# The r gate product token-major by one level of Strassen's algorithm, ahead of the branch gates

## The chip, the cores and the metric

The kernel runs on one core of one Trainium2 chip. The metric is the time of one execution on the device in microseconds (us), the median of several runs; smaller is better. The core has five engines with a queue each: PE (TensorE, matrix products and transposes; PEld is its loading of the stationary operand), DVE (VectorE), ACT (ScalarE), POOL (GpSimd) and SP (SyncE). Each engine works its instructions off in order. Matrix products read from SBUF and write to PSUM, in banks of 128 x 512 floats; DVE and ACT read PSUM. Loads from DRAM are issued here by SP, and by POOL and ACT in places.

## The reference, cut to what matters

One layer of a token mixer and a channel mixer over 512 tokens of width 1024, in fp32. `h` is the input x, normalised by its RMS and modulated by a vector computed from c (`w_ada`). One wide product `z = h @ w_in` is split into u, vs, q, r, ga, gb, k, v, lr. Then:

```python
a = _spatial_gating(gelu(u), gelu(vs), ...)          # u * (vs, normalised, mixed over tokens by sgu_w)
o, s_f, s_b = _gla_bidir(qh, k, v, lr, ...)           # gated linear attention, 4 heads of 256 values
o = o * lax.rsqrt(jnp.mean(o * o, axis=-1, keepdims=True) + EPS)
o = o.reshape(...) * gla_norm_g
ob = o * jax.nn.silu(r)
merged = jax.nn.sigmoid(ga) * (a @ w_br_a) + jax.nn.sigmoid(gb) * (ob @ w_br_b)
return merged @ w_o
```

The channel mixer follows: norm and modulation, `w_up` (44 blocks of 128 columns), a depthwise convolution over the token grid, gelu gate, `w_down`. The change concerns r, a 512 x 1024 by 1024 x 1024 product, and what is made of it, `ob`.

## The kernel before, in words

*Products.* An fp32 operand is split into a rounded part `h` and a rest `l`, both of type fp32r, and a product is three: high by high, high by low, low by high. `prod_cm` makes one block of 128 output columns for all 512 tokens, channel-major (channels on the partitions, tokens along the row): 8 slices of the inner dimension by 3 = 24 matmuls of 128x512 into one bank (L366). `wide_tm` makes blocks token-major, 128 tokens by 512 channels (L384). Activations in channel-major form (`hx` for the modulated x, 8 pairs; `a_act`; `ob`; `mg`) are the inputs of both.

*Weights.* All weights pass through one stream, in the order of the list `specs`: SP loads a raw block of 512 KB (`stream_load`, L220, 4 buffers), ACT casts it to `wh` (L232) and DVE subtracts to get `wl` (L233; 5 buffers of each). `weights()` hands out the next block and issues the splits and loads of those after it. A block is a 128-column strip with all 1024 rows, or, for the token-major products, 256 rows by 512 columns.

*Opening.* SP loads x, then, in turn, the first half of `w_ada` in groups (L282) and the first weights. For each group PE multiplies by the columns of c and c_ctx (L569), a small product sorts the result (L578), DVE makes scale and shift of it, and ACT and DVE modulate the transposed x with them (L599, L600) and split it into `hx`. Meanwhile PE already runs the first products with the parts of `hx` that are there (L660). POOL loads small rows and the decay weights (`rest_load`, L309 to L313). All of this is kept in written order.

*Stages around the change*, by the start of their products: VS (vs, token-major, `wide_tm`), U (246 us), GA/BRA (302 us: ga block, then the product of `a` with `w_br_a`, eight times), R (394 us), GB/BRB (439 us), `w_o` (524 us), the up product and convolution of the FFN (583 us) and its down product (812 us). The last is already done by Strassen's algorithm: seven products of quarters (L1554) whose weight sums POOL builds in DRAM by DMAs, plain and accumulating (`sums_build`, L201 and L203), one step with each call of `weights()` from weight 60 (`SUMS0`) on.

*U.* For each j: the product, gelu on ACT (L1226), and one step later `sgu_part`: four matmuls of 128x128 (two passes each, L1213) of the normalised vs (`vsn`, made by 32 operations on DVE, L1143) with the mixing weights, then two DVE operations (L1215, L1217) and the split of `a` (L358, L359). Between them stand, for each head, `o_scale` (the RMS factor on o, L1152) and `o_turn`: 8 transposes of 128x128 of o (L1158) and, on ACT, the factor `gng` (L1161) into a channel-major tile `ot`.

*R.* For each j a product of `prod_cm`, sigmoid on ACT (L1262), two multiplications on DVE (L1263 by `ot`, L1264 by r itself), and the split into `ob` (L358, L359).

*ada2* computes the second half of the modulation vector on DVE: 64 times a loaded tile of `w_ada` (256 KB, on SP, L1181) times a column of c, added up (L1182). It is cut into 88 steps; `tick(n)` does n of them. It starts in U; each product of U, GA/BRA, R and GB/BRB does `tick(2)`.

*Pools.* `heap` has 44 tiles of 2 KB per partition, `late` 27; PSUM has 4 banks `mm` and 4 banks `gl`. A tile that is asked for waits until the one that had its place is no longer read. The framework's scheduler sets the order of each engine's queue from the program, with some stretches kept in written order.

Of the kernel before, what the change touches and what calls it, by code (L numbers as in the profile page):

```python
# [20 lines left out]
KT = 8  # L21
# [13 lines left out]
SUMS0 = 60  # L35
# [3 lines left out]
def backbone_kernel(  # L39
# [98 lines left out]
    def w_cols(w, c0, n=P, k0=0, kn=KT):  # L138
        specs.append((w[k0 * P:(k0 + kn) * P, c0:c0 + n].rearrange("(k p) c -> p k c", p=P), kn, n))
# [24 lines left out]
    for f in range(FT):  # L164
        w_cols(ffn_w_up[0], f * P)
        w_cols(ffn_w_up[0], FF + f * P)
    quarter = lambda b, row, col: ffn_w_down[0][(4 * b + 2 * row) * P:(4 * b + 2 * row + 2) * P,
                                                 col * 512:(col + 1) * 512]
    sums = [[dp.tile([2 * P, 576], F32, name=nm("sum"))[:, :512] for _ in range(4)]
            for _ in range(BLOCKS)]  # L170

    def w_block(ap):
        specs.append((ap.rearrange("(k p) c -> p k c", p=P), 2, 512))

# [17 lines left out]
    def sums_build():  # L192
        for step in (((0, (0, 1)), (1, (1, 1)), (2, (1, 0)), (3, (0, 1))), ((0, (0, 0)), (3, (1, 1))),
                     ((1, 0),), ((2, 1),)):
            for b in range(BLOCKS):
# [14 lines left out]
    building = sums_build()  # L210
# [39 lines left out]
    def weights():  # L250
        i = pos[2]
        pos[2] += 1
        if i >= SUMS0:
            next(building, None)
        stream_split(i + 2)
        stream_load(i + 1 + AHEAD)
        return splits.pop(i)
# [519 lines left out]
    in_order(STRICT, T.engine, A.engine, V.engine)  # L777
    lsb = [heap([P, S], F32R, s="lsb") for _ in range(2)]
# [333 lines left out]
    vsn = [heap([P, 4, P], s="vsn") for _ in range(8)]  # L1112
# [28 lines left out]
    for g in range(8):  # L1141
        for t in range(4):
            V.tensor_scalar(vsn[g][:, t, :], vraw[g // 4][t][:, (g % 4) * P:(g % 4 + 1) * P], mv[:, t, 0:1],  # L1143
                            vrs[:, t:t + 1], op0=ALU.subtract, op1=ALU.mult)


    o_t = []

    def o_scale(h):
        for t in range(4):  # L1150
            ov = o_tok[h][t // 2][:, t % 2, :]
            V.tensor_scalar(ov, ov, ors[:, h, t:t + 1], None, op0=ALU.mult)  # L1152

    def o_turn(h):
        for hv in range(2):
            ps = gl()
            for t in range(4):
                T.transpose(ps[:, t * P:(t + 1) * P], o_tok[h][t // 2][:, t % 2, hv * P:(hv + 1) * P], ident)  # L1158
            t_ = late([P, S], s="ot")
            j = 2 * h + hv  # L1160
            A.mul(t_, ps, gng[:, j:j + 1])  # L1161
            o_t.append(t_)
# [42 lines left out]
    bg.append(ada2())  # L1205


    a_act = []

    def sgu_part(j, ug):  # L1210
        ps = gl()
        for t in range(4):
            T.matmul(ps[:, t * P:(t + 1) * P], vsn[j][:, t, :], swT[j // 4][:, j % 4, :], start=True, stop=True)  # L1213
# [4 lines left out]
        a_act.append(split_act(ug, s="a"))  # L1218

    prev = None  # L1220
    for j in range(KT):
        w = weights()
# [10 lines left out]
        if j < NH:  # L1233
            o_scale(j)
        if 0 < j <= NH:
            o_turn(j - 1)
        tick(2)
# [3 lines left out]
    t1, ob = [], []  # L1241
    for j in range(KT):
# [5 lines left out]
        tick(2)  # L1248
# [5 lines left out]
        tick(2)  # L1254


    for j in range(KT):
        w = weights()
        ps = mm()
        prod_cm(ps, w, hx)  # L1260
        sr = heap([P, S], s="sr")
        A.activation(sr, ps, AF.Sigmoid)  # L1262
        V.tensor_tensor(sr, o_t[j], sr, op=ALU.mult)  # L1263
        V.tensor_tensor(sr, ps, sr, op=ALU.mult)  # L1264
        ob.append(split_act(sr, s="ob"))
        tick(2)
# [3 lines left out]
    for j in range(KT):  # L1270
# [5 lines left out]
        tick(2)  # L1276
# [5 lines left out]
        mg.append(split_act(sgb_, s="mg", lo_pool=late))  # L1282
        tick(2)
# [386 lines left out]
```

## Time and profile before

| | before |
|---|---|
| median of 3 runs | 925.48 us (925.4 to 925.8) |
| profiled execution: span | 925.1 us |
| profiled execution: its own time | 928.11 us |
| granted TensorE clock | 0.998 |
| PE / DVE / ACT / POOL busy | 910.6 / 683.8 / 403.6 / 42.5 us |
| moved by DMA | 140.76 MB, 152 GB/s in the mean |

The profile is one execution, recorded by the hardware. Its times start with the first instruction; its own time is the whole execution's and includes what lies before and after the span. A row of a group reads: line, engine, operation, what it writes <- what it reads, shape, count | busy us in all, mean ns of one | idle time of the engine before them, and what ended most of it. A row of waits reads: who waits <- for whom: us in all, times, longest. A row of the chain reads: start, length, engine and line, count. A row of windows reads: stretch, its length, busy time of PE, PEld, DVE, ACT and POOL (count), granted clock, busy share of the DMA engines, GB/s. A row of one line or tile reads: line, engine, operation, count: shortest/median/longest ns, first and last start in us, shape. Matmuls are pipelined: a duration of theirs overlaps the next one's.

### The profile page before, as it was taken

The numbers are of one execution on the slowest core, as the hardware profiler recorded it, in microseconds if no ns is written. First come the engines' busy times: TensorE is split into PE (matmuls) and PEld (weight loads), VectorE is DVE, ScalarE is ACT, GpSimd is POOL, SyncE is SP. The second block draws the span as 40 slices with busy tenths as digits, with TensorE's granted clock in tenths as the row PEclk, the third lists the DMA queues.
The fourth block names the chain that finished last, engine by engine and source line by source line (L and its number), as shares of the span: only waits on it lengthen the run. The fifth ranks groups of instructions, "written<-read, shape, count | busy, mean of one in ns | idle before, by whom it ended". The sixth has DMA issues, their size and how long they took to land.

```text
span 925.1 us, 12162 instructions
## 1 busy us (share of the span) xinstructions
PE 910.6 (98%) x4540; PEld 760.5 (82%) x4540; DVE 683.8 (74%) x1187; ACT 403.6 (44%) x673; POOL 42.5 (5%) x74
## 2 busy tenths in 40 slices
PE   7999999999999999999999999999999999999996
PEld 5778888888888888888888889888888888888885
DVE  5578687779799653498575446898787778998966
ACT  5357465556542332222233236633333334467633
POOL 1200000000000000000000110011111000000000
PEclk9999999999999999999999999999999999999999
DMA  8940400511417653484444681688989632356552
GB/s 266 353 149 28 134 24 1 176 52 47 125 59 232 195 186 92 126 286 120 149 162 157 205 301 48 196 219 173 215 177 204 141 109 92 103 173 202 160 159 91
DMA packets 158615, 140.76 MB, mean 152 GB/s; under 512 B 6825, under 2 KB 122869, under 8 KB 158557
## 3 DMA queue, kind: packets, MB, share of 16 engines
q1 hardware_dynamic: 149197, 117.72, 41.1%
q0 software_dynamic: 8672, 21.19, 10.3%
q10 hardware_dynamic: 688, 1.09, 0.3%
q8 instruction: 35, 0.57, 0.2%
q14 instruction: 23, 0.19, 0.1%
HBM read 137.88 MB, written 23.07 MB: 174 GB/s over the span
## 4 chain that ended last, share of the span: by engine, by line
PE 97%; DMA 1%; ACT 0%; SPq 0%; DVE 0%; issue 0%; ACTq 0%
PE mm L366 56%; PE mm L384 12%; PE gl L1554 9%; PE gl L890 3%; PE mm L660 2%; PE mm L1554 1%; PE gl L660 1%; PE mm L997 1%; PE mm L1047 1%; PE gl L384 1%; PE gl L569 1%; PE gl L925 1%; PE gl L1213 1%; DMA wa<-in_w_ada_dram 1%; PE gl L366 1%; PE mm L377 1%
## 5 line engine op out<-in xcount | busy, mean ns | idle before, releaser
L232 ACT CAST wh<-raw 128x1024 fp32r<-128x1024 f32 x154 | 161.8, 1054 | 319.9 <-PE mm L366 204.7
L233 DVE TENSOR_TENSOR wl<-raw,wh 128x1024 fp32r<-128x1024 f32 x154 | 187.1, 1221 | 92.0 <-ACT wh L232 91.3
L366 PE MATMUL mm<-h2l,wh 128*128 128x512 f32 (+1 forms) x344 | 133.0, 387 | 0.0
L366 PE MATMUL mm<-h2h,wh 128*128 128x512 f32 (+1 forms) x344 | 133.0, 387 | 0.0
L366 PE MATMUL mm<-h2h,wl 128*128 128x512 f32 (+1 forms) x344 | 133.0, 387 | 0.0
L1401 DVE SCALAR_TENSOR_TENSOR cacc<-ca,ccol,cacc 128x441 f32<-128x441 f32 (+2 forms) x176 | 121.8, 694 | 4.1
L366 PE MATMUL mm<-hxh,wh 128*128 128x512 f32 x296 | 116.1, 392 | 0.0
L366 PE MATMUL mm<-hxl,wh 128*128 128x512 f32 x296 | 115.4, 390 | 0.0
L366 PE MATMUL mm<-hxh,wl 128*128 128x512 f32 x296 | 115.4, 390 | 0.0
L366 PEld LDWEIGHTS mm<-h2l,wh 128*128 128x128 f32 x344 | 64.6, 188 | 13.2
L366 PEld LDWEIGHTS mm<-h2h,wh 128*128 128x128 f32 x344 | 64.6, 188 | 13.2
L366 PEld LDWEIGHTS mm<-h2h,wl 128*128 128x128 f32 x344 | 64.6, 188 | 13.0
L366 PEld LDWEIGHTS mm<-hxh,wl 128*128 128x128 f32 x296 | 55.6, 188 | 11.6
L366 PEld LDWEIGHTS mm<-hxh,wh 128*128 128x128 f32 x296 | 55.6, 188 | 11.2
L366 PEld LDWEIGHTS mm<-hxl,wh 128*128 128x128 f32 x296 | 55.6, 188 | 11.2
L1182 DVE SCALAR_TENSOR_TENSOR acc<-wa,cs,acc 128x512 f32<-128x512 f32 x64 | 46.0, 744 | 3.2 <-DMA wa<-in_w_ada_dram 3.2
L1554 PE MATMUL gl<-wh,dah 128*128 128x512 f32 x120 | 46.7, 389 | 0.0
L1554 PE MATMUL gl<-wl,dah 128*128 128x512 f32 x120 | 46.7, 389 | 0.0
L1554 PE MATMUL gl<-wh,dal 128*128 128x512 f32 x120 | 46.7, 389 | 0.0
L1402 ACT ACTIVATE cacc<-cacc 128x512 f32<-128x512 f32 x22 | 13.9, 632 | 50.1 <-DVE cacc L1401 50.1
L384 PE MATMUL mm<-wh,hxh 128*128 128x512 f32 x88 | 34.7, 394 | 0.0
L384 PE MATMUL mm<-wl,hxh 128*128 128x512 f32 x88 | 34.4, 391 | 0.0
(425 smaller groups left out, 1678.8 us busy)
## 6 DMA issues: line engine op xcount, KB each, us to landing
raw<-in_w_in_dram SPq DMA_DIRECT2D x52, 512.0 KB, 3.8
wa<-in_w_ada_dram SPq DMA_DIRECT2D x96, 256.0 KB, 4.9
raw<-in_ffn_w_up_dram SPq DMA_DIRECT2D x44, 512.0 KB, 4.3
sum<-in_ffn_w_down_dram POOLq DMA_DIRECT2D x30, 512.0 KB, 6.0
raw<-sum SPq DMA_DIRECT2D x20, 512.0 KB, 3.8
raw<-in_ffn_w_down_dram SPq DMA_DIRECT2D x17, 512.0 KB, 3.5
sum<-sum POOLq DMA_DIRECT2D x10, 512.0 KB, 7.3
raw<-in_w_br_a_dram SPq DMA_DIRECT2D x8, 512.0 KB, 5.3
```

The lines of the kernel that those rows point to most:

```text
L232: A.copy(wh, raw)
L233: V.tensor_tensor(wl, raw, wh.bitcast(F32), op=ALU.subtract)
L366: T.matmul(ps, a[:, k, :], b[:, c0:c0 + n], start=(k == 0 and i == 0), stop=(k == KT - 1 and i == 2))
L377: T.matmul(ps, a[:, k, :], b[:, c0:c0 + n], start=(k == 0 and i == 0), stop=(k == KT - 1 and i == 2))
L384: T.matmul(ps, a[:, t * P:(t + 1) * P], b[:, k % 2, :], start=(k == 0 and i == 0), stop=(k == KT - 1 and i == 2))
L569: T.matmul(aps[32 * j:32 * j + 32, :cg], cs[:, k, :], wa[2 * (k // nk) + kind][:, k % nk, :], start=(k < 2), stop=(k >= KT - 2), tile_posi ...
L660: T.matmul(fps[i], a, b, start=(k == 0 and z == 0), stop=(k == KT - 1 and z == 2))
L890: T.matmul(ps, p_, q_, start=(start and z == 0), stop=(stop and z == 2))
L1182: V.scalar_tensor_tensor(acc[j], w_, cs[:, k, 0:1], acc[j], op0=ALU.mult, op1=ALU.add)
L1401: V.scalar_tensor_tensor(o, a_[:, r0 + dy:r1 + dy, c0 + dx:c1 + dx], wcol(tap), o, op0=ALU.mult, op1=ALU.add)
L1402: A.activation(acc, acc, AF.Gelu)
L1554: T.matmul(ps, a, w[:, kk, c0:c0 + n_], start=(first and kk == 0 and i == 0), stop=(last and kk == 1 and i == 2), skip_group_check=True)
```

## The change

- r is computed token-major by one level of Strassen's algorithm: the 512 x 1024 by 1024 x 1024 product is cut into two blocks of the inner dimension, each block's operands into quarters; seven products (`r_product`), each over both blocks, in place of eight. One product is 2 banks (token tiles of 128) x 2 blocks x 2 slices x 3 matmuls of 128x512 = 24. Results go to `rX` (2 banks of `mm`), `rZ` (2 of `gl`), `rY` (2 of `mm`); `taken` copies a result out on ACT, `combine` adds two on DVE.
- Its weights are 14 blocks of 256 x 512; half of them are sums of quarters that POOL builds in DRAM (a second list of 16 DMA steps of the same `sums_build`, from weight 2 on, i.e. during the attention heads and VS). For r they stand between those of U and GA.
- The sums of the other operand: each modulated tile of x (`fx`) is stored to DRAM by POOL in the opening stage; in U `hx_sum` loads quarters of it on SP (16 loads of 128 KB), adds or subtracts them on DVE and splits them.
- The RMS factor, the gate and o are combined token-major: `r_gate` does a sigmoid on ACT, two DVE operations of 128x256 (o times its factor times the sigmoid) and one of 128x512 (times r). `ob_turn` transposes the result (16 transposes for each half of the channels), multiplies by `gng` on ACT and takes the rest on DVE: that gives `ob`. `o_scale` and `o_turn` go.
- `vsn` becomes 8 operations of 128x512 in place. The high halves of `a` and `mg` are cast on ACT instead of DVE.
- R moves ahead of GA/BRA. `ada2` starts after it, with `tick(3)` in GA/BRA and GB/BRB alone. `SUMS0` is 66, since six weight blocks more stand ahead of it; the place in the program is the same.

PE at the end of r: before, r's first product follows the last of BRA's (`mm_4003`), 24 matmuls to a bank:

```order
L366 MATMUL mm_4003<-ah_3382,wh_3946 128x512
L366 MATMUL mm_4003<-al_3383,wh_3946 128x512
L366 MATMUL mm_4003<-ah_3382,wl_3947 128x512
L366 MATMUL mm_4003<-ah_3400,wh_3946 128x512
L366 MATMUL mm_4003<-al_3401,wh_3946 128x512
L366 MATMUL mm_4003<-ah_3400,wl_3947 128x512
L366 MATMUL mm_4041<-hxh_430,wh_3997 128x512
L366 MATMUL mm_4041<-hxl_431,wh_3997 128x512
L366 MATMUL mm_4041<-hxh_430,wl_3998 128x512
L366 MATMUL mm_4041<-hxh_485,wh_3997 128x512
L366 MATMUL mm_4041<-hxl_486,wh_3997 128x512
L366 MATMUL mm_4041<-hxh_485,wl_3998 128x512
```

Now GA's first product follows r, and with it stand transposes of the gated tiles (`obt`) into `gl` banks, of which the third set waits for the bank of the first:

```order
L379 MATMUL mm_3708<-hxl_546,wh_3622 128x512
L379 MATMUL mm_3708<-hxh_545,wl_3623 128x512
L379 MATMUL mm_3708<-hxh_605,wh_3622 128x512
L1289 MATMUL gl_3670<-ident,obt_3468 128x128
L1289 MATMUL gl_3670<-ident,obt_3475 128x128
L1289 MATMUL gl_3670<-ident,obt_3606 128x128
L1289 MATMUL gl_3670<-ident,obt_3611 128x128
L379 MATMUL mm_3708<-hxl_606,wh_3622 128x512
L1289 MATMUL gl_3679<-ident,obt_3468 128x128
L1289 MATMUL gl_3679<-ident,obt_3475 128x128
L1289 MATMUL gl_3679<-ident,obt_3606 128x128
L1289 MATMUL gl_3679<-ident,obt_3611 128x128
```

The transposes of o, which stood between U's products, now lie here and after BRA's first product; r is over before GA begins.

DVE in r: before, the gate's operations and splits alternate with `ada2`'s (`acc`):

```order
L1182 SCALAR_TENSOR_TENSOR acc_3982<-wa_868_4077,cs,acc_3982 128x512
L233 TENSOR_TENSOR wl_4216<-raw_4129,wh_4215 128x1024
L1263 TENSOR_TENSOR sr_4066<-ot_3021,sr_4066 128x512
L1182 SCALAR_TENSOR_TENSOR acc_3985<-wa_876_4119,cs,acc_3985 128x512
L1264 TENSOR_TENSOR sr_4066<-mm_4041,sr_4066 128x512
L1182 SCALAR_TENSOR_TENSOR acc_3988<-wa_877_4122,cs,acc_3988 128x512
L358 CAST obh_4070<-sr_4066 128x512
L1182 SCALAR_TENSOR_TENSOR acc_3979<-wa_885_4164,cs,acc_3979 128x512
L359 TENSOR_TENSOR obl_4071<-sr_4066,obh_4070 128x512
L1182 SCALAR_TENSOR_TENSOR acc_3982<-wa_886_4167,cs,acc_3982 128x512
L1263 TENSOR_TENSOR sr_4111<-ot_3028,sr_4111 128x512
```

Now, at the end of r, the last gates (`obt`), the splits of GA's and BRA's weights (`wl`), the rests of `ob_turn` and the last two combinations stand in this order:

```order
L245 TENSOR_TENSOR wl_3703<-raw_3620,wh_3702 128x1024
L1281 TENSOR_TENSOR obt_3611<-mm_3345,obt_3611 128x512
L245 TENSOR_TENSOR wl_3757<-raw_3626,wh_3756 128x1024
L245 TENSOR_TENSOR wl_3834<-raw_3706,wh_3833 128x1024
L245 TENSOR_TENSOR wl_3876<-raw_3760,wh_3875 128x1024
L1292 SCALAR_TENSOR_TENSOR obl_3658<-gl_3652,vec_b,obh_3657 128x512
L1292 SCALAR_TENSOR_TENSOR obl_3667<-gl_3661,vec_b,obh_3666 128x512
L1292 SCALAR_TENSOR_TENSOR obl_3676<-gl_3670,vec_b,obh_3675 128x512
L1292 SCALAR_TENSOR_TENSOR obl_3685<-gl_3679,vec_b,obh_3684 128x512
L1302 TENSOR_TENSOR dc_3688<-gl_3346,dt_3516 128x512
L1302 TENSOR_TENSOR dc_3695<-gl_3347,dt_3518 128x512
L1279 SCALAR_TENSOR_TENSOR obt_3690<-o_2133,var,obt_3690 128x256
```

`ada2` is gone from this stretch, and two weight splits that take the buffers of r's last product stand ahead of the first `obl`.

SP in U: before, the weights of the coming products and `ada2`'s loads:

```order
L220 DMA raw_3109<-in_w_in_dram 128x8x128
L220 DMA raw_3178<-in_w_in_dram 128x8x128
L220 DMA raw_3243<-in_w_in_dram 128x8x128
L1175 DMA acc_2935<-in_b_ada_dram 1x512
L1175 DMA acc_2938<-in_b_ada_dram 1x512
L1175 DMA acc_2941<-in_b_ada_dram 1x512
L1175 DMA acc_2944<-in_b_ada_dram 1x512
L1181 DMA wa_647_2947<-in_w_ada_dram 128x512
```

Now U's and r's weights with the first quarters of `fx` between them:

```order
L1223 DMA fq_2895<-fx_974 128x256
L1223 DMA fq_2895<-fx_976 128x256
L232 DMA raw_3141<-in_w_in_dram 128x8x128
L232 DMA raw_3191<-in_w_in_dram 128x2x512
L232 DMA raw_3241<-in_w_in_dram 128x2x512
L232 DMA raw_3291<-sum_135 128x2x512
L232 DMA raw_3354<-sum_139 128x2x512
L232 DMA raw_3360<-in_w_in_dram 128x2x512
L1223 DMA fq_3120<-fx_978 128x256
```

The loads of `ada2` have left this stretch, and the quarters' loads stand ahead of U's last weight.

The diff, cut to its core:

```diff
+    R_AT = len(specs)
...
-    for j in range(KT):
-        w_cols(wi, O_R + j * P)
...
+    quarter, sums = quarters(ffn_w_down[0], 0), sum_tiles(BLOCKS)
+    r_quarter, r_sums = quarters(wi, O_R), sum_tiles(2)
+    down_specs, specs = specs, []
+    for f in (lambda b: r_quarter(b, 0, 0), lambda b: r_sums[b][0], lambda b: r_quarter(b, 1, 0),
+              lambda b: r_sums[b][1], lambda b: r_sums[b][3], lambda b: r_sums[b][2],
+              lambda b: r_quarter(b, 1, 1)):
+        for b in range(2):
+            w_block(f(b))
+    down_specs[R_AT:R_AT] = specs
+    specs = down_specs
...
-    building = sums_build()
+    building = {SUMS0: sums_build(quarter, sums), 2: sums_build(r_quarter, r_sums)}
...
+    fx_kept = []
+    for k in range(KT):
+        d = dp.tile([P, S], F32, name=nm("fx"))
+        G.dma_start(d, fx[k])
+        fx_kept.append(d)
...
-    for g in range(8):
+    for hf in range(2):
         for t in range(4):
-            V.tensor_scalar(vsn[g][:, t, :], vraw[g // 4][t][:, (g % 4) * P:(g % 4 + 1) * P], mv[:, t, 0:1],
-                            vrs[:, t:t + 1], op0=ALU.subtract, op1=ALU.mult)
+            z = vraw[hf][t]
+            V.tensor_scalar(z, z, mv[:, t, 0:1], vrs[:, t:t + 1], op0=ALU.subtract, op1=ALU.mult)
...
+    def hx_sum(b):
+        def quad(i, hf):
+            t_ = heap([P, 2, 256], s="fq")
+            for kk in range(2):
+                dma(t_[:, kk], fx_kept[4 * b + 2 * i + kk][:, hf * 256:(hf + 1) * 256])
+            return t_
+
+        def kept(name, t_, p, q, op):
+            V.tensor_tensor(t_, p, q, op=op)
+            pair = [pool([P, 2, 256], F32R, s="xs") for pool in (heap, late)]
+            A.copy(pair[0], t_)
+            V.tensor_tensor(pair[1], t_, pair[0].bitcast(F32), op=ALU.subtract)
+            hx_sums[name, b] = pair
...
+    def r_gate(hf, t, src):
+        z = late([P, 512], s="obt")
+        A.activation(z, src, AF.Sigmoid)
+        for hh in range(2):
+            h = 2 * hf + hh
+            zh = z[:, hh * 256:(hh + 1) * 256]
+            V.scalar_tensor_tensor(zh, o_tok[h][t // 2][:, t % 2, :], ors[:, h, t:t + 1], zh,
+                                   op0=ALU.mult, op1=ALU.mult)
+        V.tensor_tensor(z, src, z, op=ALU.mult)
+        ob_t[hf, t] = z
+
+    def ob_turn(hf):
+        for jj in range(4):
+            j = 4 * hf + jj
+            ps = gl()
+            for t in range(4):
+                T.transpose(ps[:, t * P:(t + 1) * P], ob_t[hf, t][:, jj * P:(jj + 1) * P], ident)
+            hi, lo = heap([P, S], F32R, s="obh"), late([P, S], F32R, s="obl")
+            A.mul(hi, ps, gng[:, j:j + 1])
+            V.scalar_tensor_tensor(lo, ps, gng[:, j:j + 1], hi.bitcast(F32), op0=ALU.mult, op1=ALU.subtract)
+            ob[j] = (hi, lo)
...
+    def r_product(banks, ops, first=False):
+        zs = [(weights(), a) for a in ops]
+        for t in range(2):
+            for b, ((wh, wl), (hi, lo)) in enumerate(zs):
+                for kk in range(2):
+                    for i, (a, w) in enumerate(((hi, wh), (hi, wl), (lo, wh))):
+                        T.matmul(banks[t], a(kk, t), w[:, kk, :], start=(first and b == 0 and kk == 0 and i == 0),
+                                 stop=(b == 1 and kk == 1 and i == 2), skip_group_check=True)
+
+    rX, rZ, rY = ([bank() for _ in range(2)] for bank in (mm, gl, mm))
...
+    r_product(rX, r_quad(0, 0), True)
+    m1 = [taken(z) for z in rX]
...
+    r_product(rZ, ops["p1"], True)
+    m5 = [taken(z) for z in rZ]
+    r_product(rY, r_quad(1, 0), True)
+    for t in range(2):
+        r_gate(0, t, combine(rY[t], m1[t], ALU.add))
...
+    r_product(rX, ops["s2"])
+    u2 = [taken(z) for z in rX]
+    r_product(rX, ops["s3"])
+    e22 = [combine(m, z, ALU.subtract) for m, z in zip(m5, rX)]
...
+    r_product(rX, r_quad(1, 1))
+    for t in range(2):
+        r_gate(1, t + 2, e22[t])
+    for t in range(2):
+        r_gate(0, t + 2, rX[t])
+    r_product(rZ, ops["q4"])
+    ob_turn(0)
+    for t in range(2):
+        r_gate(1, t, combine(rZ[t], u2[t], ALU.subtract))
+    bg.append(ada2())
...
         t1.append(sga)
-        tick(2)
...
+        if j == 0:
+            ob_turn(1)
+        tick(3)
```

More of the change, by code (lines that the diff above doesn't have):

```diff
@@ L1253, in backbone_kernel @@
         t1.append(sga)
[L1254 to L1266, printed above, removed]
+        if j == 0:
+            ob_turn(1)
+        tick(3)
     mg = []
```

85 lines of the change are left out of this document (49 added, 36 removed).

## The prediction

> **What bounds the kernel now.** I read the engine totals first, then what TensorE waited for, then the chain of work that ended last, then the stretches around the change.
>
> ```profile
> PE 910.6 (98%) x4540; PEld 760.5 (82%) x4540; DVE 683.8 (74%) x1187; ACT 403.6 (44%) x673; POOL 42.5 (5%) x74
> ```
>
> ```profile
> PE mm L421 <- DMA rows<-in_b_ada_dram: 6.5, 1, 6.5
> PE gl L660 <- ACT hxh L599: 0.3, 1, 0.3
> PE mm L660 <- ACT wh L539: 0.2, 1, 0.2
> ```
>
> ```profile
> 300.68 1.78 PE gl L1213 x16
> 302.46 54.42 PE mm L366 x240
> ...
> 380.73 97.97 PE mm L366 x432
> ...
> 524.35 21.76 PE mm L384 x96
> ...
> 583.14 228.51 PE mm L366 x1008
> 811.65 40.80 PE gl L1554 x180
> ```
>
> TensorE is busy for 98% of the span; it waits 7.0 us, all in the opening stage (second fence; the rest of what is missing from 100% is the tail). The chain (start, length, what) consists almost only of its matmuls. So the middle of the kernel costs what its matmuls cost, and the chain gives the true price of one: 54.42/240, 97.97/432, 228.51/1008 = 0.2267 to 0.2268 us, the same for the token-major forms (21.76/96 at L384, 40.80/180 at L1554, the Strassen product of the FFN). The durations of about 390 ns elsewhere overlap. A 128x128 one of L1213 costs 1.78/16 = 0.111 us.
>
> ```profile
> 252.00:305.00 53.00, 53.00 (x286) 45.57 (x285) 49.65 (x102) 19.63 (x27) 0.00 (x0) 1.00 0.48 151
> 305.00:394.00 89.00, 89.00 (x393) 73.42 (x393) 43.26 (x54) 25.42 (x31) 2.11 (x4) 1.00 0.48 149
> 394.00:439.00 45.00, 45.00 (x200) 37.28 (x199) 40.94 (x61) 12.38 (x16) 0.00 (x0) 1.00 0.66 207
> 439.00:527.00 88.00, 88.00 (x389) 72.61 (x388) 49.82 (x69) 23.82 (x30) 3.93 (x7) 1.00 0.51 164
> ```
>
> These are the U, GA/BRA, R and GB/BRB stages (length; busy PE, PEld, DVE, ACT, POOL; clock; DMA share, GB/s). PE is full in all four at clock 1.00. The next engine is DVE, at 49.65 of 53 and 40.94 of 45 us: it hides, but with little to spare exactly where the change adds work.
>
> **The change, part by part.**
>
> *Fewer matmuls.* R was 8 products of 24 matmuls = 192; it becomes 7 products of 2 blocks x 12 = 168, all of 128x512. 24 x 0.2267 = **5.44 us** less on the engine that sets the end. The 32 transposes of o become 32 of the gated tiles, and the 64 passes of L1213 stay: nothing either way.
>
> [...]
>
> *Weight blocks.* R's weights come in 14 blocks of 512 KB instead of 8: six more loads, casts and subtractions.
>
> ```profile
> L232 ACT CAST wh<-raw 128x1024 fp32r<-128x1024 f32 x154 | 161.8, 1054 | 319.9 <-PE mm L366 204.7
> L233 DVE TENSOR_TENSOR wl<-raw,wh 128x1024 fp32r<-128x1024 f32 x154 | 187.1, 1221 | 92.0 <-ACT wh L232 91.3
> L1182 DVE SCALAR_TENSOR_TENSOR acc<-wa,cs,acc 128x512 f32<-128x512 f32 x64 | 46.0, 744 | 3.2 <-DMA wa<-in_w_ada_dram 3.2
> ```
>
> That is 6 x 1.054 = 6.3 us on ACT and 6 x 1.221 = 7.3 us on DVE. The cover: ACT is at 12.38 of 45 in R, and DVE loses L1182 there, 16.0 us in the stretch 394 to 439, whose rows (that one's groups) are:
>
> ```profile
> L1182 DVE SCALAR_TENSOR_TENSOR acc<-wa,cs,acc 128x512 f32<-128x512 f32 x22 | 16.0, 743 | 0.2 <-DMA wa<-in_w_ada_dram 0.2
> L1264 DVE TENSOR_TENSOR sr<-mm,sr 128x512 f32<-128x512 f32 x8 | 5.5, 685 | 0.1
> L358 DVE CAST obh<-sr 128x512 fp32r<-128x512 f32 x8 | 3.4, 421 | 0.1
> L1262 ACT ACTIVATE sr<-mm 128x512 f32<-128x512 f32 x8 | 4.7, 588 | 0.0
> ```
>
> DVE in the new R: 14 x 1.221 = 17.1; six combinations (L1302) at 0.685 = 4.1 and, of the eight gates, 16 half-width operations, not shown before, between a 128x256 scale at 0.344 (below) and the 0.744 of full width, taken 0.42 = 6.7, plus 8 x 0.685 = 5.5; first half of `ob_turn` 4 x 0.744 = 3.0; in all **36.4 us**, against 168 x 0.2267 = 38.1 of PE: 96%. Without the two last combinations and gates, which fall into GA, it is 31.9, or 84%. Before, R had 91%. So nothing shows at the bound on the mean; what decides is the order in DVE's queue.
>
> *Where PE waits for that queue.* A product holds both its weight blocks to its end, of five buffers. When it ends, two are free; the second is needed one product and a quarter later (its half of the first bank), 5.44 + 1.36 = 6.8 us. Cast, cast, subtract, subtract on an idle pair of engines is 1.05 + 1.05 + 1.22 = 3.3 us: 3.5 us for whatever DVE has ahead (a gate is 1.5). The bank of a product that is reused at once (`rX` after s2 and after s3) is needed half a product, 2.72 us, after its last matmul: copy on ACT 0.58, or combination on DVE 0.69 with one subtraction of 1.22 ahead of it. The last gates of `rX` (a sigmoid of 0.59 and 1.5 us on DVE for the later bank) have the 5.44 us of q4. All fit.
>
> ```profile
> L1579 ACT COPY dt<-gl 128x512 f32<-128x512 f32 x6 | 3.5, 580 | 0.4 <-PE gl L1554 0.3
> L1161 ACT ACTIVATE ot<-gl,vec_b 128x512 f32<-128x512 f32 x8 | 5.2, 688 | 4.9 <-PE gl L1158 4.9
> L1152 DVE TENSOR_SCALAR o<-o,var 128x256 f32<-128x256 f32 x16 | 5.4, 344 | 0.0
> L1143 DVE TENSOR_SCALAR vsn<-vr,mv,var 128x128 f32<-128x128 f32 x32 | 8.3, 337 | 0.0
> L600 DVE TENSOR_SCALAR xT<-xT,am,bm 128x512 f32<-128x512 f32 x7 | 3.8, 546 | 0.2
> ```
>
> The tightest place is `ob_turn(0)`. Two gl banks are held by q4's result until the combinations behind it, so its third set of transposes waits for the subtraction of the first. Two weight splits that q4's buffers release stand ahead of that subtraction on DVE. Counted from q4's last matmul: second cast to 1.25 (latency taken as 0.2), its subtraction to 2.47, `obl` at 0.744 to **3.21**; PE gets there after 8 x 0.111 + 10 x 0.2267 = **3.16**. The next set comes at 3.96 against 3.9. Bounds: 0 if DVE's intervals are a tenth shorter than its durations; 1.2 if one more split is late; I take **+0.2 us**. Behind those transposes on PE stands the rest of GA's first product; its sigmoid on ACT and the release of its weight buffer wait for that, with some 10 us of split weights in hand.
>
> *What leaves and enters elsewhere.* vsn: 32 x L1143 (8.3 us) becomes 8 of 128x512, nearest L600, 4.4 us; `o_scale` (5.4) goes; U gains 8 sums and 8 subtractions at 0.69 (11.0) and 8 casts on ACT, whose 19.63 of 53 covers them; the a and mg casts (8 each, 0.42) go from DVE to ACT. L1182's 16 of U (11.9) leave. DVE in U: 49.65 - 11.9 - 5.4 - 3.4 + 11.0, and two more splits (2.4), 42 of the 52.6 us that are left of the stage. Price 0; without that cover PE would wait at L1213's step for a gl bank.
>
> ```profile
> raw<-in_w_in_dram SPq DMA_DIRECT2D x52, 512.0 KB, 3.8
> wa<-in_w_ada_dram SPq DMA_DIRECT2D x96, 256.0 KB, 4.9
> ...
> sum<-in_ffn_w_down_dram POOLq DMA_DIRECT2D x30, 512.0 KB, 6.0
> raw<-sum SPq DMA_DIRECT2D x20, 512.0 KB, 3.8
> ...
> sum<-sum POOLq DMA_DIRECT2D x10, 512.0 KB, 7.3
> ```
>
> *DMA of R.* Sixteen sums on POOL start with weight 2 and end with weight 17, the last of VS; the first is loaded seven weights later, about 38 us at 5.44 each, against a landing of 7.3: price 0. The 16 reloads (128 KB) sit on SP ahead of U7's weight and of R's sixth block and wait for tiles of the heap; their data lie in DRAM since long. Bounds 0 and 1 if one holds the sixth block; 0 taken. R moves 14 x 0.524 MB in 38.1 us = 193 GB/s, below the 207 that R ran with.
>
> *The eight stores of modulated x* (256 KB each, POOL) fall into the opening. Its rows: windows as above, then the ada weights (L282) with their reader L569, with start and landing times, the modulation L600, and POOL's later loads with their first reader.
>
> ```profile
> 24.00:28.00 4.00, 4.00 (x47) 3.05 (x46) 1.08 (x4) 1.02 (x2) 0.00 (x0) 1.00 1.07 324
> ```
>
> ```profile
> L282 SPq DMA_DIRECT2D wa<-in_w_ada_dram x8: 432/506/1156, 17.1 to 24.3; - x8
> ...
> DMA to landing us min/median/max: 3.9/3.9/3.9
> ```
>
> ```profile
> L569 PE MATMUL gl<-wa,cs x32: 272/273/298, 29.5 to 30.4; 128*32 128x128 f32 x32
> ...
> DMA to landing us min/median/max: 4.5/4.6/4.7
> ```
>
> ```profile
> L600 DVE TENSOR_SCALAR xT<-xT,am,bm x7: 540/546/550, 22.3 to 55.2; 128x512 f32<-128x512 f32 x7
> ```
>
> ```profile
> L313 POOL DMA_DIRECT2D w2r<-in_gla_w_dram x6: 484/488/521, 33.4 to 37.4; - x6
> ...
> L697 DVE CAST w2s<-w2r x2: 422/423/424, 47.6 to 48.7; 96x512 fp32r<-96x512 f32 x2
> ```
>
> DMA is full there (share 1.07 at 324 GB/s), so a store pushes every later load by 0.262 MB / 324 GB/s = 0.81 us. The ada weights issued until 24.3 land at 24.3 + 3.9 to 4.6 = 28.2 to 28.9 and are read from 29.5: 0.6 to 1.3 us to spare. Two stores (the first x tile, and the one that L600 writes at 22.3) come before: 1.6 us. PE, full there, stalls 0.3 to 1.0; bounds 0 (the writes find room) and 2.4 (all of three); I take **+0.7 us**. The next group was read later after its landing by more than 2 us and takes the third store without a stall. Three stores also stand ahead of POOL's small loads: 37.4 + 3 x 0.6 + 5.3 = 44.5 against 47.6: price 0.
>
> *ada2 moved.* Its 64 loads and L1182 leave U and R for GA/GB, three per weight instead of two: 3 x 0.262 + 0.524 MB in 5.44 us = 241 GB/s, above 207. Each loaded tile holds one of about five late slots (8 t1, 8 obl, 4 acc, 2 g1 of 27): 5 per (4.9 landing + 0.744 + up to two splits of 1.221 = 8.1 us) is 0.62 per us, 0.55 needed. R had 22 in 45, 0.49, with 0.2 us of waits. Price 0; DVE per pair of products is 2 x 1.22 + 6 x 0.744 + 0.69 = 7.6 of 10.9.
>
> *Sum.* Profiled execution: span 925.1 - 5.44 + 0.2 + 0.7 = 920.6; its own time 928.11 becomes 923.6. The median, 925.48, lies 2.6 below that run; less the same 4.54 it is **920.9 us** (-0.49%). A measurement of this kernel tells about 0.2%, 1.85 us, from no change.
>
> **Rivals.**
>
> 1. *More is given back*, still within the saving: the opening costs its 2.4, and the hand-offs (bank reuse, `ob_turn` twice) one subtraction of 1.22 more: 920.9 + 1.7 + 1.2 = 923.8. For: DVE's 96%, the full DMA. Against: PE waited nowhere in before's R, at 91%.
>
> 2. *Slower: R is paced by its weight splits.* DVE's queue is in order, and in all it waited 91.3 us for casts (L233's row). If the first split of each product stands exposed for its cast, 7 x 1.054 = 7.4 us join DVE's 36.4: 43.8 instead of 38.1 for R, 920.9 + 5.7 = 926.6; with the second cast exposed too, 51.2, and 934. It decides where DVE's work and waits in R pass 38.1 + 4.54 = 42.6 us. Against: a wait costs nothing while splits are ahead.
>
> 3. *Slower: ada2 starves in GA/GB.* At 11 us per slot instead of 8.1 a weight's three loads take 6.6 us, the 64 of them 21 x 1.16 = 25 us more than PE leaves; three to four weights in hand hide about 18: +7, 928. It decides near 10.7 us. For: 241 GB/s was never sustained so long. Against: L1182 waited 3.2 us for wa in all.
>
> 4. *The saving is larger*: the opening and `ob_turn` cost nothing and the tail falls well, 919.2 to 920.0 and less.
>
> **How the numbers follow.** Forecast (920.0 to 922.4): 0.50. Rival 1: 0.19, a third of it above 923.6. Rival 2: 0.16, a third of it within 0.2%. Rival 3: 0.06, slower. Rival 4: 0.09. Faster: 0.50 + 0.13 + 0.09 = 0.72; same 0.06 + 0.05 = 0.11; slower 0.11 + 0.06 = 0.17. The range 919.2 to 927.0 leaves out the upper parts of 2 and 3 (0.15) and a little of 4 (0.03).
>
> **What would show it.** Right: a stretch of 168 matmuls of the R line in the chain in 38.1 us; PE waits of some tenths on `obl` at the transposes and of under 1 us on `wa` (or L569's chain) before 50 us, and none in U, GA, GB. Wrong: PE waits on weight subtractions or on `dc` in R (1, 2), DVE waits on wa above 10 us in GA/GB (3), or a matmul interval of the new product other than 0.2267.

## The result and the profile after

The changed kernel runs in 922.48 us (median of 6 runs, 921.8 to 922.79) against 925.75 (6 runs, 925.4 to 926.4): ratio 0.9964, 95% interval 0.9951 to 0.9976, 3.3 us less. Measured again, beside eleven runs of before, it was 922.31 against 926.44, ratio 0.9954 (0.9942 to 0.9966), 4.1 us less. The forecast was 920.9, with a range of 919.2 to 927.0.

First the engine totals of the changed kernel, then what its PE waited for:

```profile
PE 906.7 (98%) x4516; PEld 756.7 (82%) x4516; DVE 688.7 (75%) x1159; ACT 427.4 (46%) x709; POOL 58.5 (6%) x98
```

```profile
PE mm L434 <- DMA rows<-in_b_ada_dram: 5.6, 1, 5.6
PE gl L1124 <- DVE swl L372: 0.3, 1, 0.3
...
```

PE has 24 instructions fewer, is as full as before, and waits in the middle at one new place: in U, for `swl`, the rest of the split mixing weights (second row). That stands for more than its 0.3 us, as will be seen. The chain of the changed kernel around r (start, length, what):

```profile
299.61 5.46 PE mm L1311 x24
305.07 5.44 PE gl L1311 x24
310.51 21.76 PE mm L1311 x96
332.27 5.44 PE gl L1311 x24
337.71 0.87 PE gl L1289 x8
...
340.87 0.61 PE gl L1289 x4
...
341.71 0.44 PE gl L1289 x4
```

The 168 matmuls of r follow each other without a gap from 299.61 to 337.71: 38.1 us, 0.2268 each, as forecast. Behind them stands `ob_turn(0)`: its third set of transposes takes 0.61 instead of the 0.44 of the fourth, a stall of 0.17 us.

How long an execution takes from its start to the first full product of the heads varies from run to run by more than a microsecond (that product starts between 89.58 and 91.10 us in twelve of the thirteen profiles, and at 94.13 in that with all stores doubled). So the parts are compared from that product's first matmul to the last matmuls of the kernel. The fences give these two rows of the chain, of before, of a second profile of it, of the changed kernel, and of a second profile of that:

```profile
91.05 5.47 PE mm L366 x24
...
916.37 1.37 PE gl L1510 x6
```

```profile
90.08 5.47 PE mm L366 x24
...
915.43 1.37 PE gl L1510 x6
```

```profile
90.97 5.47 PE mm L379 x24
...
911.85 1.37 PE gl L1601 x6
```

```profile
90.45 5.47 PE mm L379 x24
...
910.53 1.37 PE gl L1601 x6
```

The distance, called the body below, is 825.32 and 825.35 us in before, 820.88 and 820.08 in the changed kernel: 4.45 and 5.26 us less. The 24 matmuls are worth 5.44 and `ob_turn` takes 0.17 back, which leaves 5.27: the second profile shows just that, the first one has lost another 0.8 us, in U. From the first matmul of `w_o` to that last row all four take 392.02 us, so the differences lie ahead of it. The heads' product starts between 90.1 and 91.05 in all four. Of the two profiles of the changed kernel the first is the typical one: its execution took 922.44 us, at the median, while the second took 921.13 where the median of its runs is 922.31.

### The profile page after: what moved, and what is told of

Read it like the earlier page. It is cut to its first block, busy times and chain, and to the rows that moved or that the text cites. A ratio compares the mean times of both kernels' runs of the same rounds, so it can differ in the third digit from the quotient of the medians.

```text
span 920.7 us, 12269 instructions
## 1 busy us (share of the span) xinstructions
PE 906.7 (98%) x4516; PEld 756.7 (82%) x4516; DVE 688.7 (75%) x1159; ACT 427.4 (46%) x709; POOL 58.5 (6%) x98
## 4 chain that ended last, share of the span: by engine, by line
PE 97%; DVE 1%; DMA 1%; ACT 1%; issue 0%; ACTq 0%; DVEq 0%; SPq 0%
PE mm L379 51%; PE mm L397 12%; PE gl L1645 9%; PE gl L909 3%; PE mm L1311 3%; PE mm L673 2%; PE mm L1645 1%; PE gl L673 1%; PE mm L1016 1%; PE mm L1066 1%; PE gl L397 1%; PE gl L1311 1%; PE gl L582 1%; PE gl L944 1%; PE mm L546 1%; PE gl L1210 1%
## 5 line engine op out<-in xcount | busy, mean ns | idle before, releaser
L244 ACT CAST wh<-raw 128x1024 fp32r<-128x1024 f32 x160 | 168.1, 1054 | 266.0 <-PE mm L379 130.6
L245 DVE TENSOR_TENSOR wl<-raw,wh 128x1024 fp32r<-128x1024 f32 x160 | 194.2, 1220 | 79.7 <-ACT wh L244 74.0
L379 PE MATMUL mm<-hxh,wh 128*128 128x512 f32 x232 | 91.2, 393 | 0.0
L379 PE MATMUL mm<-hxh,wl 128*128 128x512 f32 x232 | 90.5, 390 | 0.0
L379 PE MATMUL mm<-hxl,wh 128*128 128x512 f32 x232 | 90.5, 390 | 0.0
L1182 DVE SCALAR_TENSOR_TENSOR acc<-wa,cs,acc 128x512 f32<-128x512 f32 x64 | 44.6, 746 | 12.8 <-DMA wa<-in_w_ada_dram 12.8
L379 PEld LDWEIGHTS mm<-hxh,wl 128*128 128x128 f32 x232 | 43.5, 188 | 9.2
L379 PEld LDWEIGHTS mm<-hxh,wh 128*128 128x128 f32 x232 | 43.6, 188 | 8.7
L379 PEld LDWEIGHTS mm<-hxl,wh 128*128 128x128 f32 x232 | 43.6, 188 | 8.6
## 6 DMA issues: line engine op xcount, KB each, us to landing
wa<-in_w_ada_dram SPq DMA_DIRECT2D x96, 256.0 KB, 5.0
```

What stands on the lines that cost most here:

```text
L244: A.copy(wh, raw)
L245: V.tensor_tensor(wl, raw, wh.bitcast(F32), op=ALU.subtract)
L379: T.matmul(ps, a[:, k, :], b[:, c0:c0 + n], start=(k == 0 and i == 0), stop=(k == KT - 1 and i == 2))
L1182: V.scalar_tensor_tensor(acc[j], w_, cs[:, k, 0:1], acc[j], op0=ALU.mult, op1=ALU.add)
```

## The experiments

The theory was the forecast's, with two corrections that the trace after suggested: the stores in the opening cost nothing (PE reads the ada weights at 29.55 us, as before at 29.61), and U lost 0.8 us. The runs come from three chips, each with its own runs of before; a time of one chip beside a time of another is a weaker comparison than the two ratios.

**The kernel before, profiled again** (no edit).

> The kernel before, unchanged, profiled a second time: the first profile of it lasted 928.11 us with a span of 925.1, while its other runs have a median of 925.75; the changed kernel's profiled run (922.44, span 920.7) agrees with its median. Theory: the first profile was a long one by about 1 us and a second has a span near 924.0 and a time near 925.7, so that the change saved 3.3 us and not 4.4. Rival: the span is again 925.1, and what lies around the span differs between the two kernels.

Measured: 925.85 us, span 924.1, as the theory had it. Eleven more runs of it on that chip have spans of 923.9 to 925.4 and times 1.7 to 2.0 us above them; of 21 runs on another chip four lie 2.5 to 2.9 above. So the first profile's time, 3.0 us above its span, was a long one for what lies outside the span. Its body was not: it is that of the second.

**The changed kernel again** (no edit).

> The changed kernel, unchanged, timed in the same session as the next two. Expected 922.5 us, 3.3 us below the kernel before.

Measured: 922.31 us (920.89 to 923.4), 4.1 below before. Its profile has no wait for `swl` at all: the 0.8 us in U come and go from run to run.

It shows something else. These are PE's reads of the ada weights in the opening, 32 matmuls each, in the first profile of the changed kernel and in this one:

```profile
24.91 1.01 PE gl L582 x32
29.55 1.01 PE gl L582 x32
36.47 1.86 PE gl L582 x32
```

```profile
23.74 1.35 PE gl L582 x32
28.72 1.01 PE gl L582 x32
35.66 2.14 PE gl L582 x32
```

The read that the prediction named (second row) takes 1.01 us in both, but here the one ahead of it and the one behind it are held for 0.34 and 0.28 us. The waits do not list this. Of the seven profiles with the eight stores as they are, this one loses 0.6 us in this way, that of the last experiment below 0.3, and five lose nothing; neither do the four profiles without stores (before twice, the order alone, no stores).

**Sums later in U.**

```diff
     for j in range(KT):
-        next(pieces[j])
         w = weights()
...
         prev = (j, ug)
+        next(pieces[j])
```

> The changed kernel with each step of hx_sum written at the end of its turn of U instead of at its start, so that DVE normalises vs and makes swl before the first sums, whose loads arrive at 250 us. Theory: U lost 0.8 us because DVE stood 1.4 us waiting for these loads with the normalisation behind them, and PE then waited for swl at 259.9; without it the time falls by 0.8 us against the changed kernel, to 921.7. Rival: the wait only moves (R waits for its first sums, or DVE is the bound of U anyway): no change or slower.

Measured: 921.2 us (920.75 to 921.96), ratio 0.9946 (0.9933 to 0.9958); body 820.09. DVE at the start of U, in the changed kernel's first profile, then in this one (start, length, line, operation, count, and in brackets the idle time before it):

```profile
249.08 0.69 DVE L1227 TENSOR_TENSOR fq<-fq,fq 128x512 f32<-128x512 f32 x1 [1.12 <-DMA fq<-fx]
250.03 0.69 DVE L1227 TENSOR_TENSOR fq<-fq,fq 128x512 f32<-128x512 f32 x1 [0.26 <-DMA fq<-fx]
...
251.38 3.73 DVE L1162 TENSOR_SCALAR vr<-vr,mv,var 128x512 f32<-128x512 f32 x8
...
259.17 0.68 DVE L372 TENSOR_TENSOR swl<-swT,swh 128x512 fp32r<-128x512 f32 x1
```

```profile
248.72 3.75 DVE L1162 TENSOR_SCALAR vr<-vr,mv,var 128x512 f32<-128x512 f32 x8
...
254.71 1.29 DVE L372 TENSOR_TENSOR swl<-swT,swh 128x512 fp32r<-128x512 f32 x2
```

In the changed kernel the first sums stand in DVE's queue ahead of the normalisation and wait for their reloads; `swl` is ready at 259.85. PE's instructions there, in the changed kernel's first profile and in its second:

```profile
257.85 0.40 PE L1124 MATMUL gl<-swh,ones_r 128*128 128x512 f32 x1
...
259.90 0.50 PE L1124 MATMUL gl<-swl,ones_r 128*128 128x512 f32 x1 [0.33 <-DVE swl L372]
...
260.38 0.48 PE L379 MATMUL mm<-hxh,wh 128*128 128x512 f32 x1
```

```profile
257.36 0.40 PE L1124 MATMUL gl<-swh,ones_r 128*128 128x512 f32 x1
...
259.10 0.48 PE L379 MATMUL mm<-hxh,wh 128*128 128x512 f32 x1
```

From the first of these matmuls to U's third product pass 2.53 us in the one and 1.74 in the other: the whole 0.8. The recorded wait is less than that, since the ends of matmuls are modelled. With the sums later `swl` is ready at 256.0, and PE has no wait in r either. The loss goes with the landing of the first reloads in all eight profiles that have the sums where the change puts them. In three they land 3.0 to 3.1 us after their issue, DVE waits 0.3 to 0.6 us for them, and PE loses nothing. In four they take 3.9 to 4.1, DVE waits 1.4 to 1.5, and U loses 0.8 to 0.9. In one they take 4.7, DVE waits 2.0, and U loses 1.5. With the sums later they take 4.1 and, in the last experiment, 5.1, and U loses nothing. So the wait's mechanism is shown; the medians differ by 1.1 us, more than the 0.8 of the stretch, but the ranges of the runs overlap.

**Stores twice.**

```diff
         fx_kept.append(d)
+        d2 = dp.tile([P, S], F32, name=nm("fx2"))
+        G.dma_start(d2, fx[k])
```

> The changed kernel with each of the eight stores of modulated x done twice, the second into a tile that nobody reads (2.1 MB more written in the opening). The theory of the prediction was that a store there pushes the loads of the ada weights by 0.81 us and PE with them: then two to three more stores ahead of the read at 29.5 us cost 1.5 to 2.5 us, +2 us. Rival, by the profile after, where the same read starts at 29.55 us against 29.61 before: the stores find room, the time stays within 0.3 us of the changed kernel.

Measured: 924.05 us (922.68 to 925.71), 1.7 above the changed kernel. The profiled execution is the slowest of the seven. From its waits of PE between 20 and 60 us, and its chain:

```profile
PE gl L582 <- DMA wa<-in_w_ada_dram: 0.9, 3, 0.4
```

```profile
94.13 5.47 PE mm L379 x24
...
915.08 1.37 PE gl L1603 x6
```

The heads' product starts 3.2 to 3.7 us later than in the changed kernel's two profiles, and PE waits three times for ada weights: the read that begins at 29.34 us is held for 1.2 us, the next one for 2.1. Not all of that need be the stores': SP's loads were 0.95 us behind those of the changed kernel's first profile (L317 at 16.16 us against 15.21) before the first store went out at 18.40. So PE can stall there, as the prediction had it, and doubling all eight stores costs 1.7 us by the medians, though the ranges of the runs overlap (the changed kernel's go up to 923.4).

**The first two stores twice** (the same edit under `if k < 2`).

> The changed kernel with only the first two of the eight stores done twice. With all eight doubled PE waited three times for ada weights (0.9 us recorded) and the 300th matmul started 3.2 us later. Theory: a store pushes the loads by its share of the DMA time and the group read at 29.5 us has 1.5 to 2 us of room, which the two single stores use up; two more, 1.6 us, then cost 1 to 2 us. Rival: what costs is the later stores (third to fifth): then under 0.5 us.

Measured: 922.8 us (922.46 to 923.09); the heads' product starts at 90.87, within the scatter of the changed kernel. No cost in the opening: four stores (18.60 to 23.49 us) go out ahead of the read at 29.38, and it takes 1.01 us as before. With all eight doubled the same four were ahead and that read was held, so their number alone does not decide it; whether it was the later stores or the lag of that execution's loads stays open. (This profile has the longest wait for `swl`, 1.0 us in two pieces, and a body of 821.62.)

**No stores.**

```diff
-        d = dp.tile([P, S], F32, name=nm("fx"))
-        G.dma_start(d, fx[k])
-        fx_kept.append(d)
+        fx_kept.append(x[0, (k % 4) * P:(k % 4 + 1) * P, (k // 4) * S:(k // 4 + 1) * S])
```

> The changed kernel without the eight stores of modulated x; the sums read the same shapes from the input x instead (so r is not what the reference has, while every load, sum and product of it stays). Theory after the doubling, which cost 3.5 us in the opening: single stores stay inside the room that the ada weights' loads have, so leaving them out gains nothing: within 0.5 us of the changed kernel's 922.3, and the 300th matmul starts at 42.5 to 43.5 us as before. Rival (the prediction's +0.7): 0.7 us or more faster.

Measured: 922.45 us (920.82 to 923.09); the heads' product at 90.14, body 820.07. The sums read the input x instead. Leaving the eight stores out does not lower the median. From the second read of the ada weights to the heads' product pass 71.2 us in this profile, in the two of before, in that of the order alone, and in five of the seven with the eight stores; the two with a held read take 71.5 and 71.8. So most of the scatter of the opening arises before 20 us, where in those seven at most one store has gone out.

**A product more in r.**

```diff
-        for t in range(2):
+        for t in [t for t in range(2) for _ in range(times)]:
...
-    r_product(rX, ops["s2"])
+    r_product(rX, ops["s2"], times=2)
```

> The changed kernel with the 24 matmuls of the product s2 issued twice (its result doubled, so r is not what the reference has). Theory: R is bound by PE and a product costs 24 x 0.2267 us, so the time is 5.4 us above the changed kernel's 922.3, near 927.7, the time of the kernel before. Rival (R is paced by weight splits or DVE): the added matmuls hide in part and cost less than 4 us.

Measured: 927.19 us, 4.9 above the changed kernel (922.31 above), ratio to before 1.0011 (1.0002 to 1.002). Its body is 826.38, with the wait for `swl`, 5.50 us above that of the changed kernel's profile that has that wait too (820.88). From its chain in r, which begins at 298.34:

```profile
309.24 27.20 PE mm L1311 x120
336.44 5.44 PE gl L1311 x24
```

r ends at 341.88, after 43.54 us instead of 38.10: the 24 matmuls cost 5.44 us, 0.2267 each, and nothing of them hides. PE sets the pace of r.

**More DVE work in r.**

```diff
+        for z in banks:
+            V.tensor_tensor(spare, z, spare, op=ALU.mult)
```

> The changed kernel with two more DVE operations of 128x512 behind each product of r, which read its banks and whose result nobody uses: 14 x 0.69 = 9.7 us more DVE work in R, 46.1 by the prediction's sum against 38.1 of PE. By the prediction's second rival R is then paced by DVE: at most 46.1 - 38.1 = 8.0 us are lost, less what is split ahead and what runs on into GA; I expect 2 to 6 us lost, and PE waits on wl, dc or dt there. If R had more room than the sum says, under 1 us.

Measured: 921.8 us (921.1 to 923.71), body 820.03: nothing lost, where 2 to 6 us were expected. The windows of r, of the changed kernel and of this one (stretch, length; busy PE, PEld, DVE, ACT, POOL; clock; DMA share, GB/s):

```profile
299.00:337.00 38.00, 38.00 (x172) 31.56 (x171) 29.40 (x41) 22.31 (x29) 2.11 (x4) 1.00 0.51 153
```

```profile
299.00:337.00 38.00, 38.00 (x173) 31.56 (x172) 34.27 (x51) 23.28 (x29) 2.05 (x4) 1.00 0.47 141
```

DVE is at 29.4 of 38, not at 36.4: in that stretch stand 13 splits (15.8 us), 12 half-width operations (5.2), four combinations and six full-width ones of the gates (6.9) and 4.3 us of U's end, by durations that overlap a little; `ob_turn` and the last gates come behind it. Even 34.3 of 38 leaves PE no wait. The added operations also read the banks, and the copies `dt` that free a bank now wait for them (3.9 us in five waits; in the changed kernel they wait for PE alone); that too costs PE nothing.

**Twice that** (four operations behind each product).

> As the run with more DVE work in r, but with four operations behind each product instead of two, 28 in all. The fourteen added 4.9 us of DVE time to the stretch of r (29.4 to 34.3 of 38.0) and cost nothing. Twenty-eight are 19.2 us: 29.4 + 19.2 = 48.6, above 38.1. Theory (PE waits only when the queue's work passes PE's time and the blocks split ahead are used up): 3 to 10 us lost, with PE waits on wl or dc in r. If it still costs under 1 us, the work spills into GA and the lead of the weights covers it.

Measured: 928.76 us (925.16 to 930.79), 6.4 above the changed kernel; body 826.13. PE where it stands in r, with what it waited for in brackets, and then the row of the chain behind it:

```profile
322.77 0.73 PE L1311 MATMUL gl<-wh,xs 128*128 128x512 f32 x2 [1.18 <-ACT wh L244]
323.34 0.38 PE L1289 MATMUL gl<-ident,obt 128*128 128x128 f32 x2
325.44 0.67 PE L1311 MATMUL mm<-wh,xs 128*128 128x512 f32 x1 [1.72 <-ACT dt L1297]
```

```profile
325.44 4.61 PE mm L1311 x12
```

The product ahead of this ends at 321.60. PE waits 1.18 us for the cast of a weight block, does two matmuls and two transposes, and waits 1.72 us for the copy `dt` that frees a bank. The next twelve matmuls take 4.61 us instead of 2.72. One such copy `dt`, in this run and in the changed kernel:

```profile
324.80 0.59 ACT L1297 COPY dt<-mm 128x512 f32<-128x512 f32 x1 [1.55 <-DVE spare L1315]
```

```profile
318.70 0.59 ACT L1297 COPY dt<-mm 128x512 f32<-128x512 f32 x1 [0.41 <-PE mm L1311]
```

Here the copy waits for the added operations on its bank, there for the product alone. So this run does two things at once: it fills DVE, and it puts DVE between a bank and its copy. It shows that PE stalls when a bank comes free too late; it does not show at what load of DVE the weight splits alone would pace r.

**The order alone**: the kernel before with R ahead of GA/BRA and ada2 moved. Its edits are the reordering of two loops and of their weights, `lo_pool=late` for `ob`, `bg.append(ada2())` behind R and:

```diff
-        tick(2)
+        tick(3)
```

> The kernel before with only the order changed: R (eight products as before, the rest of ob in late tiles) ahead of GA/BRA, and ada2 in GA/BRA and GB/BRB alone at three steps per weight. No Strassen, no stores, no sums. Theory: the matmuls are the same and the order costs nothing: within 0.5 us of the kernel before. Rival (ada2 starves at 241 GB/s, the prediction's third rival): slower by 2 us or more, with PE waits in GA/GB.

Measured: 926.98 us against 926.15, ratio 1.0008 (0.9999 to 1.0017); body 825.64, 0.3 above before's. DVE waits for `wa`, in the changed kernel and in this one:

```profile
DVE acc L1182 <- DMA wa<-in_w_ada_dram: 12.8, 8, 3.5
```

```profile
DVE acc L1182 <- DMA wa<-in_w_ada_dram: 13.5, 12, 3.4
```

The denser ada2 makes DVE wait four times as long as before (3.2). In this run one such wait reaches PE: the chain (start, length, what) leaves PE in GB and goes through a load of ada2 and DVE's work behind it.

```profile
479.79 4.64 DMA wa<-in_w_ada_dram
...
493.84 0.50 PE gl L1190
```

That last matmul adds up what ada2 made, and follows the one ahead of it after 0.50 us instead of 0.24: most of the 0.3 us of the body. The median is 0.8 above before's, and the interval includes no change. In the changed kernel's two profiles the chain stays on PE there. So the order alone saves nothing: the saving is Strassen's.

**Sums later, and ob_turn later.**

```diff
-    ob_turn(0)
...
-        if j == 0:
-            ob_turn(1)
+        if j < 2:
+            ob_turn(j)
```

> The changed kernel with the sums at the end of each turn of U and with ob_turn(0) written after GA's and BRA's first pair of products and ob_turn(1) after the second, in place of before them. Theory: the waits at ob_turn cost 0.2 us and go; with the sums later the time is 0.8 to 1.0 us below the changed kernel, 921.4, and about 5.3 us below the kernel before. Rival: the late slots that the gated tiles hold for longer starve ada2 in GA, and the time rises.

Measured: 920.93 us (920.6 to 922.62), ratio to before 0.9947 (0.9933 to 0.996), body 819.90: 0.2 us under the kernel with only the sums later, which is what the stall at `ob_turn` was worth. Its chain has no stall at the transposes: GA's first 48 matmuls follow r without a gap. Its median is the lowest, 1.4 us below that of the changed kernel (922.31), but that was taken on another chip, and beside its own runs of before it is no better than the sums later alone (0.9947 and 0.9946). That it beats the changed kernel (0.9954) is likely and not proven, the intervals overlap.

## Why the prediction was right, and where it was not

*The 24 matmuls at 0.2267 us*: right. r takes 38.1 us, adding a product costs 5.44, and the body of the undisturbed profile is 5.26 us shorter, which is 5.44 less the 0.17 of `ob_turn`. The run with a product more has 226.7 ns for one matmul (5.44/24), as the chain of before has, so the chain's interval is the one to use here.

*The stall at `ob_turn(0)`, +0.2*: right in place and size, 0.17, and it goes when `ob_turn` is written later. The 0.2 us of latency in its count was the author's estimate, and no run shows it: in the changed kernel the second cast begins 0.08 us after q4's row of the chain ends (337.79 against 337.71).

*The stores in the opening, +0.7*: wrong; 0 in most executions. The step that failed is "PE, full there, stalls 0.3 to 1.0", at the read of 29.5 us. Two stores do go out ahead of it (18.72 and 23.08 us), and in all seven profiles with the eight stores that read takes its 1.01 us; so it has more room than the prediction gave it from the landing times of a few of these loads. Two of the seven lose 0.3 and 0.6 us at the reads beside it. That the stores did this is possible and not shown: none of the four profiles without them has it, but four are few.

*U, price 0*: wrong; 0.8 to 0.9 us in four of eight profiles, 1.5 in one, 0 in three. The step added up DVE's work (42 of 52.6 us; it is 41.56 in the 53.61 from 246.00 to 299.61) and named what would happen without that cover. The sign it gave for being right, no PE wait in U, failed with it. It left out the order: the first sums stand in DVE's queue ahead of the normalisation and wait there for the first of the 16 reloads, which the paragraph on DMA had priced at 0, among others because "their data lie in DRAM since long". The data do; but the loads stand on SP behind weight blocks that wait for their buffers (SP is with four of them from 217.08 to 243.22), and go out from 243.31 us on (SP's queue: start, length):

```profile
240.19 3.03 SPq L232 DMA_DIRECT2D raw<-in_w_in_dram  x2
243.31 3.85 SPq L1223 DMA_DIRECT2D fq<-fx  x8
```

*These two errors cancel*, and that is luck: the sum of -4.54 stands beside -4.45 in the body of the first profile, but its terms should have been -5.44, +0.17 and, in U, 0 to +1.5 (there 0.8), with 0 to +0.6 in the opening.

*DVE in r, 36.4 us*: 29.4 in r itself, the rest behind it. r is not paced by DVE: with fourteen operations more, 39.0 us by their durations (29.4 + 14 x 0.685), PE loses nothing. With 28 more (48.6) it loses 5.3 us of the body, but through the hand-off of a bank and one cast, and the added operations stand in that hand-off. So rival 2 is far from the changed kernel, and its bound of 42.6 is neither confirmed nor refuted.

*ada2 in GA/GB*: the price of 0 held. The sign given for rival 3, DVE waits on wa above 10 us, appeared (12.8) and cost PE nothing: GA/BRA from its second pair on, GB/BRB and all up to `w_o` take 167.48 us in both profiles of the changed kernel, on an unbroken chain of PE. The order alone, with 13.5 us of such waits, loses 0.3. So the rival's mechanism exists, and the sign is not enough to tell that it costs.

*The medians*: 922.48 and 922.31 lie 1.4 to 1.6 above the forecast. Part is the base: before's median was 925.48 in the runs shown, 925.75 and 926.44 with more, 0.3 and 1.0 us. What is left, 1.3 and 0.4 us, is not in the body, which in a typical execution is 4.45 us shorter where 4.54 was forecast. It lies in the scatter ahead of the heads' product or outside the span; why the two measurements show 3.3 and 4.1 us saved is not settled beyond that.

## What to carry to other kernels

Where one engine is full from end to end, a saving of its instructions is worth their true interval, read from a long unbroken row of the chain (here 0.2267 us a matmul), and the rest of the forecast is a list of queues. For each new instruction ask what it waits for and what stands behind it on its engine: a new operation that waits for a load need not cost anything by itself (in the run with the sums later the reloads take 4.1 us to land and U loses nothing), but ahead of something urgent it passes its wait on (1.4 us on DVE ahead of the normalisation, 0.8 of U lost). When saturated transfers (here a DMA share of 1.07 at 324 GB/s) are near a critical read, double the new load and take it away before calling it a cost, and look at the length of the reads in several profiles: one held read of 0.3 us stands in no list of waits.

## What the runs showed of the hardware that was not expected

In the run with 28 more operations PE did 0.7 us of work in 3.84 us, from 321.60 to 325.44, and its next twelve matmuls took 4.61 us instead of 2.72. The windows of that run (the granted clock is the third number from the end):

```profile
322.70:323.75 1.05, 0.95 (x4) 0.57 (x4) 0.47 (x2) 0.55 (x2) 0.00 (x0) 1.00 0.03 8
323.75:325.40 1.65, 0.00 (x0) 0.00 (x0) 1.65 (x5) 0.59 (x1) 0.00 (x0) 1.00 0.00 0
...
327.00:328.00 1.00, 1.00 (x3) 0.75 (x3) 1.00 (x3) 0.27 (x1) 0.00 (x0) 0.50 0.00 0
328.00:328.90 0.90, 0.90 (x4) 0.67 (x3) 0.83 (x1) 0.32 (x1) 0.00 (x0) 0.50 0.42 81
328.90:329.50 0.60, 0.60 (x4) 0.51 (x3) 0.00 (x0) 0.00 (x0) 0.00 (x0) 0.90 1.02 293
```

The granted clock is 1.00 in the first two rows (the work between the two waits, and the second wait), 0.50 from 327.00 to 328.90 us, 0.90 in the row behind that and 1.00 from 330.00 to 335.00; from 325.40 to 330.00 it is 0.63 in the mean. So r lost 3.2 us to the waits (3.84 less the work done) and 1.9 more while the clock was low (4.61 less 2.72), which together are the 5.1 us by which its chain through r is longer, the four transposes within it left aside. The clock is back at about 329.0 us by the row of 0.90, 3.6 us after PE went on at 325.44. PE had not stood still throughout: the longest stand was 1.72 us, and four instructions lay between it and the one of 1.18. What in such a stretch brings the clock down, and how much work keeps it up, no run here shows. A forecast of a stall on a full PE should ask for this price too (1.9 us here), also where the stall is broken by a few instructions.
